# Layer 0 of a two-layer encoder: PSUM banks read earlier, the U product beside two gate groups, the Fourier transform between the other two

## The chip, the cores and the metric

One NeuronCore of a Trainium2 chip runs the whole computation. The metric is the device time of one execution in microseconds, as the median of several runs.

## The reference

Two layers (`DEPTH = 2`) over 512 positions of width 2048, in float32. Each layer normalises `x`, scales and shifts it by a vector that a large matrix `w_ada` makes of `c`, and multiplies by `w_in`. The columns of that product are: `u_f` (1024, the input of a Fourier mixing), `z_f` (1024, its gate), `cq` (512) and `ckv` with a rotary key (256 + 64) for latent attention, and `z_a` (1024, the attention's gate).

```python
h = _layernorm(x) * (1.0 + scale[:, None, :]) + shift[:, None, :]
u_f, z_f, cq, ckv, k_r, z_a = jnp.split(h @ w_in[l], split_pts, axis=-1)
y_f = _fourier_mix(u_f, w_fmix[l]) * jax.nn.silu(z_f)
...
y_a = _mla_attention(q_nope, q_rope, k_nope, k_rope, v) * jax.nn.silu(z_a)
y = jnp.concatenate([y_f, y_a], axis=-1) @ w_out[l]
x = _layernorm(DEEPNORM_ALPHA * x + gate[:, None, :] * y, ln_g[l], ln_b[l])
```

## The kernel before

**Precision.** Every operand of a large product is held as a high and a low part. `split` (L148) makes them: ScalarE (ACT) casts the value (L149), VectorE (DVE) subtracts the cast from the value (L150). `mm3` (L152) multiplies with three matmuls (L153 to L155). Attention's small operands are made in the same way by `scaled` (L427, L428).

**Weights.** `Stream` (L56) holds the weights as a list of units in the order of use. A unit is loaded by a DMA that SyncE (SP) issues into one of three `wr` buffers and then converted; `st.ahead(raw, conv)` says how many units are loaded and converted ahead of the one in use. A `dense` unit is 256 rows of 512 columns, one cast and one subtraction of 1024 columns. A `fold_unit` (L390) is 128 rows of the 1024 `u_f` columns: DVE adds and subtracts mirrored columns (L404, L405), ACT casts, DVE subtracts (L150) and adds to a running row (L415); `first_eo` (L621), which belongs to it, prepares the matching rows of the activations (ACT L624, DVE L625 and L626, a split of 512 columns). All converted tiles, sums and activations share 35 slots of the pool `bp`.

**Layer 0.** The vector of `w_ada` is needed before `h` exists, so layer 0 runs over the 16 blocks of 128 rows of `w_in` in five steps of 1, 2, 3, 4 and 6 blocks (`SZ`, L88), while DVE works the `w_ada` sums (L250) beside them. In each step `k_group` (L1079) runs over six column groups: CQ, CKV, two of `z_f` (ZF) and two of `z_a` (ZA). A group fills four PSUM banks, and these are then read: copied by ACT in the first step (L1099), added to a sum in SBUF by DVE afterwards (L1101). CQ alone stays in PSUM over the steps. PSUM has eight banks: four named `pa`, four named `pm`.

**The last step** (six blocks, three pairs a group) has the order CQ, CKV, ZA, ZA, ZF, ZF. Beside the four gate groups runs the product U (`u_step`, L714): one step for each of 16 fold units, 24 matmuls of 252 or 260 columns into the four `pm` banks. `UPAT` (L104) says how many U steps follow each of the twelve pairs: two in the first group, four in the second, five in the third, five in the fourth. Each group's sums then go through SiLU and are spilled to DRAM by SP (`spill`). Ahead of the fourth group `next(lq)` and `next(lkv)` read the two latents back from DRAM (`lat`) and rotate the key.

**Behind the last step** (L1142 to L1155) stand: `u_finish`, which splits the four `pm` banks of U; `folded_constants`, which makes the Fourier constants with twelve full-precision matmuls (L550); the transposes of the latents (L862); and then, alternating, the Fourier transform (`fourier_folded`, 14 steps on the `pm` banks) and the rotary part of the queries (`rotary_queries`, eight tiles). `project(0)` makes keys, values and queries of the first two heads, and the attention loop follows.

**What sets the order.** The program is written as one sequence. A planner at build time ranks each instruction by its place in that sequence, simulates the engines, and gives each engine a fixed order: the instruction of the lowest rank whose operands and buffers its simulation has ready. On the chip each engine takes its instructions in that order. `tc.high_priority(offset=n)` ranks instructions as if they had been written n instructions earlier.

Of the kernel before, what the change touches and what calls it, by code (L numbers as in the profile page):

```python
# [21 lines left out]
NT = S // P  # L22
# [60 lines left out]
def trunk_kernel(ctx: ExitStack, tc: tile.TileContext, x, c, positions, w_ada, b_ada, w_in, q_norm,  # L83
# [17 lines left out]

    FW, UAH, UA0, YS = 2, 6, 3, 4

    UPAT = [0, 1, 1, 2, 1, 1, 2, 2, 1, 2, 1, 2]  # L104


    XE, RN0, PL, WL = 8, 2, 1, 2
# [322 lines left out]
    def wq_unit(l, h0, nh, off, n):  # L430
        def load():
            t = wraw([P, 4, nh, n])
            for k in range(4):
                SP.dma_start(t[:, k], w_q_b[l, k * P:(k + 1) * P, :].rearrange(
                    "p (h c) -> p h c", c=192)[:, h0:h0 + nh, off:off + n])
            return t.rearrange("p k h c -> p k (h c)")

        def conv(t):
            s = [big([P, 2, 2, nh * n]) for _ in range(2)]
            for k in range(4):  # L440
                scaled(s[k // 2][:, 0, k % 2], s[k // 2][:, 1, k % 2], t[:, k], gcol(l, k))
            return lambda a, k: s[k // 2][:, a, k % 2]
        return Unit(load, conv)
# [27 lines left out]
    for l in range(DEPTH):  # L471
        if l == 0:
            for k0, nk in STEPS:
                last, m, ku = k0 + nk == NK, 0, 0
                for g in LAST if last else FIRST:
                    for k, n in pairs(k0, nk):
                        st.add(dense(w_in[l], k * P, *g, n))
                        if last and g in ZA + ZF:
                            for _ in range(UPAT[m]):
                                st.add(fold_unit(w_in[l], ku, lambda k: first_eo(k)))  # L480
                                ku += 1
                            m += 1
            for k in range(2):
                st.add(wq_unit(l, 4 * k, 4, 128, 64))
        else:
            add_groups(w_in[l], [ZA[0], ZF[0]])
            for k in range(NK):
                st.add(fold_unit(w_in[l], k))
            add_groups(w_in[l], [ZF[1], CQ, CKV])
            for k2 in range(8):  # L490
                if k2 in (0, 4):
                    st.add(wq_unit(l, k2, 4, 128, 64))
                st.add(dense(w_in[l], k2 * 256, *ZA[1]))
        for h0 in range(0, H, 2):
            st.add(wkv_unit(l, h0))
            st.add(wq_unit(l, h0, 2, 0, 128))
        add_groups(w_out[l], [(c0, 512) for c0 in range(0, D, 512)])
        ends.append(len(st.units))

# [161 lines left out]
    for l in range(DEPTH):  # L661
# [315 lines left out]
            while pending:  # L977
                pending.pop(0)()

        def project(h0):  # L980
            wv = st.next()
            for tp in range(2):
                v = big([P, 2, 2, 256])
                ps = pa()
                for t_ in range(2):
                    tb = tp * 2 + t_
                    ts = slice(tb * P, (tb + 1) * P)
                    o = ps[:, t_ * 256:t_ * 256 + 256].rearrange("p (h c) -> p h c", h=2)
                    for k in range(2):
                        mm3(o, ckv[k][:, 0, ts], ckv[k][:, 1, ts], wv(0, k)[:, :, 1], wv(1, k)[:, :, 1],  # L990
                            k == 0, k == 1)
                split(v[:, 0], v[:, 1], ps.rearrange("p (t c) -> p t c", t=2))
                for t_ in range(2):
                    for hd in range(2):
                        vs[h0 + hd, tp * 2 + t_] = v[:, :, t_, hd * P:(hd + 1) * P]
            wq = st.next()
            for hd in range(2):
                hs = slice(hd * P, (hd + 1) * P)
                ps = pa()
                for k in range(2):  # L1000
                    mm3(ps, wv(0, k)[:, hd, 0], wv(1, k)[:, hd, 0], ckv[k][:, 0], ckv[k][:, 1], k == 0, k == 1)
                t = big([P, 2, S])
                split(t[:, 0], t[:, 1], ps)
                ks[h0 + hd] = t
                ps = pa()
                for k in range(4):
                    mm3(ps, wq(0, k)[:, hs], wq(1, k)[:, hs], cq[k][:, 0], cq[k][:, 1], k == 0, k == 3)
                t = big([P, 2, S])
                scaled(t[:, 0], t[:, 1], ps, SCALE)
                qs[h0 + hd] = t  # L1010
# [57 lines left out]
        if l == 0:  # L1068

            for step, (k0, nk) in enumerate(STEPS):  # L1070
                final = k0 + nk == NK
                if step > 0:
                    finish_late()
                for k in range(k0, k0 + nk) if step else ():
                    h[k] = make_h(0, xT[k // 2][:, k % 2], k)
                left = [0 if final else float(sum(NK // (1024 // (256 * n)) for n in chunks(STEPS[step + 1][1])))]
                pace = left[0] / (6.0 * len(pairs(k0, nk)) * LEADS[step])

                def k_group(g, banks, work=lambda: None):  # L1079
                    n = g[1]  # L1080
                    k00, k01 = (0, NK) if g == CQ else (k0, k0 + nk)
                    for k, nr in pairs(k0, nk):
                        w = st.next()
                        p_ = min(pace, left[0])
                        left[0] -= p_
                        bg_step(p_ if p_ > 0 else ZP if not final else ZL if g in (CQ, CKV) else 0)
                        if g in ZF or g in ZA:
                            fm_half(banks, w, h, k, k == k00, k + nr == k01)
                        else:
                            tm_half(banks, w, h, k, n, k == k00, k + nr == k01)  # L1090
                        work()
                    if g == CQ:
                        return banks
                    if k0 == 0:
                        sums[g] = [big([P, 2, n], F32) for _ in range(2)]
                    s_ = [sums[g][tb // 2][:, tb % 2] for tb in range(NT)]
                    for tb in range(NT):
                        if k0 == 0:
                            A.copy(s_[tb], banks[tb][:, :n])  # L1099
                        else:  # L1100
                            V.tensor_tensor(s_[tb], s_[tb], banks[tb][:, :n], op=ALU.add)  # L1101
                    return s_

                if step == 0:
                    keep = [pa() for _ in range(NT)]
                if not final:
                    for i, g in enumerate(FIRST):
                        k_group(g, keep if g == CQ else [pm() for _ in range(NT)])
                        if step == 0 and i == 3:
                            cos_t, sin_t = rotary_tables()  # L1110
                    continue

                def pas():
                    return [pa() for _ in range(NT)]

                lq = latent_q(k_group(CQ, keep))
                next(lq)
                lkv = latent_kv(k_group(CKV, pas()))
                next(lkv)
                finish_late()  # L1120
                st.ahead(4, UA0)
                ub, ku, todo_u = None, 0, iter(UPAT)

                def u_steps():
                    nonlocal ub, ku
                    for _ in range(next(todo_u)):
                        if ub is None:
                            ub = u_start()
                        u_step(ub, ku)
                        ku += 1  # L1130

                for i, (g, dst) in enumerate(zip(LAST[2:], (0, 1, 2, 3))):
                    if i == 3:
                        next(lq)
                        next(lkv)
                        raw = constants_raw(0)
                    zs = k_group(g, pas(), u_steps)
                    for j in range(4):
                        A.activation(zs[j], zs[j], AF.Silu)
                    spill(dst, zs)  # L1140
                st.ahead(4, 2)
                u = u_finish(ub)  # L1142
                cw, nq, dt = folded_constants(0, raw)
                drain(lq)
                drain(lkv)
                fb, rq = fourier_folded(u), rotary_queries(1)
                for i in range(8):
                    next(fb, None)
                    next(rq, None)
                    next(fb, None)  # L1150
                drain(fb)
                gt = gates()
        else:
            unfolded(first_group(), 0)
# [24 lines left out]
            next(rq)  # L1179
            unfolded(fm_group(last, G1), 4)  # L1180
            drain(lkv)
        project(0)
        drain(rq)
        todo = [(hd, qh) for hd in range(H) for qh in range(2)]
        es, pts = {}, {}
# [161 lines left out]
```

## Time and profile before

| | us |
|---|---|
| median of three runs | 1429.53 (1428.49 to 1431.82) |
| the profiled execution | 1431.62 |
| its span, first to last instruction | 1429.8 |

| stretch of the span | us |
|---|---|
| steps of layer 0 but the last | 31 to about 222 |
| last step: CQ and CKV | to 246.6 |
| last step: the four gate groups with U | 246.6 to 373 |
| `u_finish`, constants, Fourier, rotary queries, first projections | 373 to 449.7 |
| attention of layer 0 and output projection | 449.7 to about 720 |
| layer 1 | to 1429.8 |

How to read it: TensorE (PE) is the engine with the most work. What counts is where it has idle time and which engine's instruction ends each idle stretch. A matmul's listed duration is longer than its share of PE's time, since matmuls overlap; the distance from start to start is what one costs. The same holds in a small way for DVE.

### The profile page before, as it was taken

The page shows a single profiled execution, that of the slowest core. Times are in us where ns is not written, and L with a number is a line of the kernel's source. Part 1 is how long each engine was busy: PE and PEld are TensorE (multiplying, and loading weights), DVE is VectorE, ACT ScalarE, POOL GpSimd, SP SyncE. Part 2 cuts the span into 40 slices and gives each one's busy share as a digit, 9 for nine tenths or more (in the row PEclk, how much of TensorE's full clock was granted, in tenths as well). Part 3 has the DMA queues.
Part 4 walks back from the last instruction along what each step waited for, and adds up shares of the span by engine and source line. Part 5 has one row for each costly group of instructions (what it writes and reads, how often), then busy time and mean ns, then how long its engine had stood idle before and what let it go on. Part 6 is the DMA issues. An engine that isn't in the chain of part 4 may idle for free. (4 is left out here: it accounts for less than half of the span.)

```text
span 1429.8 us, 19111 instructions
## 1 busy us (share of the span) xinstructions
PE 1326.3 (93%) x7029; PEld 1129.9 (79%) x7029; DVE 1041.0 (73%) x1744; ACT 602.3 (42%) x1135; POOL 59.7 (4%) x95
## 2 busy tenths in 40 slices
PE   4889899989898999999997998998999999999996
PEld 3768788878677888787776887887898888888885
DVE  7799993996689898689888748447655577733448
ACT  6521333754536776211157524323134577722110
POOL 1000000000100000000031001011100000000001
PEclk9999999999999999999998998999999999999998
DMA  8889853656466346989736435349734321272312
GB/s 275 294 277 321 296 206 113 192 180 184 147 227 223 118 148 202 328 299 319 271 113 214 161 99 155 89 147 337 247 93 110 111 66 46 59 259 89 103 59 118
DMA packets 137077, 260.88 MB, mean 182 GB/s; under 512 B 19788, under 2 KB 51672, under 8 KB 136984
## 3 DMA queue, kind: packets, MB, share of 16 engines
q1 hardware_dynamic: 129944, 236.33, 50.5%
q0 software_dynamic: 7040, 23.34, 4.7%
q8 instruction: 55, 0.90, 0.3%
q14 instruction: 38, 0.31, 0.1%
HBM read 241.12 MB, written 18.50 MB: 182 GB/s over the span
## 5 line engine op out<-in xcount | busy, mean ns | idle before, releaser
L153 PE MATMUL pa<-b,b 128*128 128x512 f32 (+2 forms) x1344 | 509.8, 381 | 33.2 <-ACT b L149 13.7
L154 PE MATMUL pa<-b,b 128*128 128x512 f32 (+2 forms) x1344 | 508.6, 379 | 5.1 <-DVE ln_v L190 5.1
L155 PE MATMUL pa<-b,b 128*128 128x512 f32 (+2 forms) x1344 | 506.5, 378 | 0.5 <-DVE b L150 0.5
L153 PEld LDWEIGHTS pa<-b,b 128*128 128x128 f32 x1344 | 256.1, 191 | 82.7 <-ACT b L149 19.9
L154 PEld LDWEIGHTS pa<-b,b 128*128 128x128 f32 x1344 | 257.9, 192 | 46.5 <-DVE ln_v L190 5.3
L149 ACT CAST b<-wr 128x1024 fp32r<-128x1024 f32 (+3 forms) x166 | 162.4, 989 | 313.1 <-PE pa L155 158.2
L155 PEld LDWEIGHTS pa<-b,b 128*128 128x128 f32 x1344 | 257.3, 192 | 46.8 <-DVE b L150 2.4
L150 DVE TENSOR_TENSOR b<-wr,b 128x1024 fp32r<-128x1024 f32 (+3 forms) x166 | 188.8, 1145 | 133.2 <-PE pa L154 61.0
L250 DVE SCALAR_TENSOR_TENSOR acc<-ada,cact,acc 128x1024 f32<-128x1024 f32 (+2 forms) x193 | 226.9, 1183 | 22.5 <-DMA ada<-in_w_ada_dram 20.6
L153 PE MATMUL pm<-b,b 128*128 128x256 f32 (+5 forms) x692 | 221.5, 320 | 8.3 <-DVE b L1101 3.7
L154 PE MATMUL pm<-b,b 128*128 128x256 f32 (+5 forms) x692 | 215.8, 312 | 0.0
L155 PE MATMUL pm<-b,b 128*128 128x256 f32 (+5 forms) x692 | 215.7, 312 | 0.0
L153 PEld LDWEIGHTS pm<-b,b 128*128 128x128 f32 x692 | 132.8, 192 | 21.0 <-issue 8.6
L154 PEld LDWEIGHTS pm<-b,b 128*128 128x128 f32 x692 | 133.1, 192 | 6.9
L155 PEld LDWEIGHTS pm<-b,b 128*128 128x128 f32 x692 | 132.9, 192 | 6.6
L150 DVE TENSOR_TENSOR b<-pm,b 128x512 fp32r<-128x512 f32 (+6 forms) x120 | 66.1, 574 | 38.8 <-ACT b L149 38.3
L149 ACT CAST b<-pm 128x512 fp32r<-128x512 f32 (+5 forms) x120 | 56.6, 499 | 65.4 <-PE pm L770 29.4
L149 ACT CAST b<-b 128x1024 fp32r<-128x1024 f32 (+1 forms) x48 | 43.3, 912 | 46.9 <-DVE b L405 29.0
L150 DVE TENSOR_TENSOR b<-b,b 128x1024 fp32r<-128x1024 f32 (+1 forms) x48 | 49.6, 1044 | 15.3 <-ACT b L149 15.3
L149 ACT CAST b<-t 128x512 fp32r<-128x512 f32 (+1 forms) x81 | 40.8, 530 | 40.3 <-DVE t L1059 15.2
L150 DVE TENSOR_TENSOR b<-t,b 128x512 fp32r<-128x512 f32 (+1 forms) x81 | 45.2, 578 | 9.3 <-ACT b L149 9.3
L1027 ACT ACTIVATE t<-t,ssum 128x512 f32<-128x512 f32 x64 | 45.3, 735 | 1.7 <-DVE ssum L1026 1.7
(180 smaller groups left out, 1247.6 us busy)
## 6 DMA issues: line engine op xcount, KB each, us to landing
wr<-in_w_in_dram SPq DMA_DIRECT2D x107, 512.0 KB, 4.0
ada<-in_w_ada_dram SPq DMA_DIRECT2D x96, 512.0 KB, 5.9
wr<-in_w_out_dram SPq DMA_DIRECT2D x64, 512.0 KB, 4.8
ada<-in_w_ada_dram SPq DMA_DIRECT2D x96, 256.0 KB, 5.1
ada<-in_w_ada_dram POOLq DMA_DIRECT2D x32, 512.0 KB, 5.1
b<-in_x_dram SPq DMA_DIRECT2D x16, 512.0 KB, 6.1
t<-szd SPq DMA_DIRECT2D x32, 256.0 KB, 4.1
ada<-in_w_ada_dram SPq DMA_DIRECT2D x32, 192.0 KB, 4.0
```

The source lines that it names most:

```text
L149: A.copy(hi, src)
L150: V.tensor_tensor(lo, src, f(hi), op=ALU.subtract)
L153: PE.matmul(o, lh, rh, start=first, stop=False)
L154: PE.matmul(o, lh, rl, start=False, stop=False)
L155: PE.matmul(o, ll, rh, start=False, stop=last)
L250: V.scalar_tensor_tensor(out=a, in0=t[:, r - r0], scalar=cact[:, r:r + 1], in1=a, op0=ALU.mult, op1=ALU.add)
L1027: A.activation(e, e, AF.Copy, scale=ssum)
```

## The change

Five things, all but the last two in the last step of layer 0:

- The reads of the PSUM banks at the end of every `k_group` stand in `tc.high_priority(offset=300)`. This holds in all five steps.
- `UPAT` is 2, 3, 3, 3, 3, 2: all 16 U steps follow the six pairs of the two ZA groups.
- `u_finish` and `folded_constants` stand ahead of the first ZF group (with `st.ahead(4, 2)`), the constants' DMAs one group earlier; after each of the six pairs of the ZF groups come two steps of the Fourier transform. The rest of it stands between the transposes of the latents.
- The rotary queries no longer alternate with the Fourier transform. One step stands ahead of `project(0)`, four inside it, the rest behind it.
- The second unit of rotary query weights moves behind the first pair of projection units. `project(0, rq)` holds for layer 1 too, where one last step of `rq` is left by then.

```diff
-    UPAT = [0, 1, 1, 2, 1, 1, 2, 2, 1, 2, 1, 2]
+    UPAT = [2, 3, 3, 3, 3, 2]
+    EV = 300
...
-                        if last and g in ZA + ZF:
+                        if last and g in ZA:
...
-            for k in range(2):
-                st.add(wq_unit(l, 4 * k, 4, 128, 64))
+            st.add(wq_unit(l, 0, 4, 128, 64))
...
+            if l == 0 and h0 == 0:
+                st.add(wq_unit(l, 4, 4, 128, 64))
...
-        def project(h0):
+        def project(h0, other=iter(())):
             wv = st.next()
             for tp in range(2):
+                next(other, None)
...
             for hd in range(2):
+                next(other, None)
...
-                    for tb in range(NT):
-                        if k0 == 0:
-                            A.copy(s_[tb], banks[tb][:, :n])
-                        else:
-                            V.tensor_tensor(s_[tb], s_[tb], banks[tb][:, :n], op=ALU.add)
+                    with tc.high_priority(offset=EV):
+                        for tb in range(NT):
+                            if k0 == 0:
+                                A.copy(s_[tb], banks[tb][:, :n])
+                            else:
+                                V.tensor_tensor(s_[tb], s_[tb], banks[tb][:, :n], op=ALU.add)
...
+                fb = None
                 for i, (g, dst) in enumerate(zip(LAST[2:], (0, 1, 2, 3))):
+                    if i == 1:
+                        raw = constants_raw(0)
+                    if i == 2:
+                        st.ahead(4, 2)
+                        fb = fourier_folded(u_finish(ub))
+                        cw, nq, dt = folded_constants(0, raw)
                     if i == 3:
                         next(lq)
                         next(lkv)
-                        raw = constants_raw(0)
-                    zs = k_group(g, pas(), u_steps)
+                    zs = k_group(g, pas(), u_steps if i < 2 else runner(fb, 2))
...
-                st.ahead(4, 2)
-                u = u_finish(ub)
-                cw, nq, dt = folded_constants(0, raw)
+                next(fb, None)
                 drain(lq)
+                next(fb, None)
                 drain(lkv)
-                fb, rq = fourier_folded(u), rotary_queries(1)
-                for i in range(8):
-                    next(fb, None)
-                    next(rq, None)
-                    next(fb, None)
                 drain(fb)
+                rq = rotary_queries(1)
+                next(rq)
                 gt = gates()
...
-        project(0)
+        project(0, rq)
         drain(rq)
```

## Rows read from the trace of the kernel before

**Rows 1.** The page: busy time of each engine, share of the span, instructions.
```profile
PE 1326.3 (93%) x7029; PEld 1129.9 (79%) x7029; DVE 1041.0 (73%) x1744; ACT 602.3 (42%) x1135; POOL 59.7 (4%) x95
```

**Rows 2.** Waits of PE, 225 to 460 us: total, times, longest.
```profile
PE pa L153 <- DVE b L1101: 9.3, 3, 3.8
```

**Rows 3.** Timeline of PE, last step: start, duration, instruction, idle before it.
```profile
246.60 0.39 PE L153 MATMUL pa<-b,b 128*128 128x512 f32 x1
...
257.51 0.28 PE L153 MATMUL pm<-b,b 128*128 128x260 f32 x1
...
260.33 0.39 PE L153 MATMUL pa<-b,b 128*128 128x512 f32 x1
...
265.82 0.28 PE L153 MATMUL pm<-b,b 128*128 128x260 f32 x1
```

**Rows 4.** Timeline of PE, where the second ZA group and the ZF groups start.
```profile
303.12 0.77 PE L153 MATMUL pa<-b,b 128*128 128x512 f32 x1 [3.78 <-DVE b L1101]
...
308.28 0.40 PE L153 MATMUL pa<-b,b 128*128 128x512 f32 x1
...
339.59 0.76 PE L153 MATMUL pa<-b,b 128*128 128x512 f32 x1 [3.33 <-DVE b L1101]
...
345.70 0.40 PE L155 MATMUL pa<-b,b 128*128 128x512 f32 x1
```

**Rows 5.** Stretch of 10 us: PE, PEld, DVE, ACT, POOL busy; granted clock, DMA, GB/s.
```profile
300.00:310.00 10.00, 6.88 (x20) 5.57 (x21) 8.53 (x12) 5.67 (x10) 0.00 (x0) 0.66 0.72 215
```

**Rows 6.** Waits of PE, 373 to 391 us (first and last of five).
```profile
PE pm L755 <- ACT b L149: 2.9, 1, 2.9
...
PE pm L862 <- DVE fc L558: 0.4, 1, 0.4
```

**Rows 7.** Waits of PE, 391 to 450 us (first two and last of six).
```profile
PE pa L153 <- DVE b L150: 2.4, 1, 2.4
PE pm L970 <- ACT b L427: 2.3, 1, 2.3
...
PE pm L153 <- issue: 0.5, 1, 0.5
```

**Rows 8.** Timeline of PE: the first instruction of the attention scores.
```profile
449.71 0.39 PE L1019 MATMUL pa<-b,b 128*128 128x512 f32 x1
```

**Rows 9.** Timeline of DVE beside the ZA groups.
```profile
250.22 0.42 DVE L625 TENSOR_TENSOR t<-t 128x256 f32<-128x256 f32 x1
...
262.31 1.22 DVE L150 TENSOR_TENSOR b<-wr,b 128x1024 fp32r<-128x1024 f32 x1
...
264.05 0.68 DVE L404 TENSOR_TENSOR b<-wr 128x504 f32<-128x504 f32 x1
...
268.35 0.68 DVE L404 TENSOR_TENSOR b<-wr 128x504 f32<-128x504 f32 x1
...
271.95 1.88 DVE L1101 TENSOR_TENSOR b<-b,pa 128x512 f32<-128x512 f32 x3
```

**Rows 10.** Timeline of DVE: a wait for the latents, one behind a spill, bank reads.
```profile
330.40 0.19 DVE L872 TENSOR_TENSOR t<-b,cos_t 128x32 f32<-128x32 f32 x1 [6.08 <-DMA b<-lat]
...
348.34 0.68 DVE L404 TENSOR_TENSOR b<-wr 128x504 f32<-128x504 f32 x1 [2.09 <-DMA szd<-b]
...
363.57 0.69 DVE L1101 TENSOR_TENSOR b<-b,pa 128x512 f32<-128x512 f32 x1 [2.83 <-PE pa L155]
364.94 0.69 DVE L1101 TENSOR_TENSOR b<-b,pa 128x512 f32<-128x512 f32 x1 [0.69 <-PE pa L155]
```

**Rows 11.** Busy time by stretch: layer 1's group with the Fourier steps between its pairs.
```profile
922.00:985.00 63.00, 62.97 (x332) 53.23 (x331) 37.17 (x63) 17.78 (x35) 8.96 (x17) 1.00 0.56 186
```

**Rows 12.** DVE by line and shape, 371 to 450 us: count, busy, mean ns.
```profile
L250 DVE SCALAR_TENSOR_TENSOR acc<-ada,cact,acc 128x1024 f32<-128x1024 f32 x18 | 23.0, 1279 | 0.0
```

**Rows 13.** Busy time by stretch, attention and output projection (first, last of four).
```profile
450.00:500.00 50.00, 49.97 (x297) 43.71 (x296) 44.78 (x83) 39.12 (x84) 0.00 (x0) 1.00 0.46 153
...
600.00:700.00 100.00, 96.59 (x432) 78.26 (x432) 90.78 (x98) 17.90 (x17) 0.00 (x0) 1.00 0.89 315
```

**Rows 14.** Waits of PE, 0 to 240 us: the steps before the last.
```profile
PE pm L153 <- DVE b L1101: 3.7, 3, 2.0
```

## The prediction

> **What bounds the kernel now.** I read the page's busy times first: PE is busy 93% of the span, DVE 73% [rows 1]. So the question for any part of this kernel is where PE stands idle. I then took the waits of PE in the stretch that the change rewrites, and the timelines of PE and DVE there. In this stretch, from the first ZA matmul at 246.60 [rows 3] to the first score at 449.71 [rows 8], 203.1 us long, the losses are of three kinds.
>
> First, the starts of the second, third and fourth gate group wait for the bank reads of the group before: 9.3 us in three waits [rows 2]. PE has only four `pa` banks, and the reader sees why the reads are late: DVE has the conversions of units ahead in front of them. After the two longer waits the clock is down. [...] The twelve matmuls from 303.12 to 308.28 took 5.16 us [rows 4]. At full clock a dense pair of 24 matmuls takes 265.82 - 260.33 = 5.49 us [rows 3], 0.229 each, so twelve take 2.75: 2.4 us lost. From 339.59 to 345.70 [rows 4] it is 14 matmuls in 6.11 instead of 3.2: 2.9 us. Together these starts cost 9.3 + 5.3 = 14.6 us.
>
> Second, behind U, 373 to 391 us: five kinds of waits, 2.9 us for the split of U's banks and down to 0.4, sum 6.0 [rows 6]. Nothing else was left for PE there.
>
> Third, 391 to 450 us, the Fourier steps beside the rotary queries: six kinds, 2.4 and 2.3 down to 0.5, sum 9.2 [rows 7].
>
> From 450 us PE is busy 49.97 of 50 us [rows 13], so what is saved before that shifts everything after it.
>
> **The change, part by part.**
>
> *Group starts (gain 13.5).* The ranks move the bank reads ahead of conversions, and the new pattern puts three U steps behind the last pair of the first ZA group and two behind that of the second. A U step is 260.33 - 257.51 = 2.82 us [rows 3], so the reads have 8.5 and 5.6 us of PE work over them and need four times 1.88 / 3 = 0.63 us [rows 9], 2.5 us. Both waits go, with their clock loss. The start of the second ZF group has two Fourier steps over it, and DVE there has the latents behind the reads now: its 6.08 us wait for them [rows 10] stays but holds up no fold unit. I leave 1 us. Bounds: 9.3 (the clock falls elsewhere) to 14.6.
>
> *U in half the time (loss 6.5).* This is the part that costs. PE's work for the two ZA groups is 6 x 5.49 + 16 x 2.82 = 78.1 us: from 246.60 to 324.7. DVE takes 268.35 - 264.05 = 4.30 us for one fold unit with its activations, back to back [rows 9]. So it needs 16 x 4.30 = 68.8, five dense units of 1.22 and eight bank reads of 0.63: 79.9 us. It gets to them at 250.22 [rows 9], behind the latents; the first fold unit now stands one place nearer in the stream, and I take its 4.30 as done by then, in DVE's idle time beside CKV. That gives 250.22 + 75.6 = 325.8 and 2.82 for the last U step: 328.6, 3.9 us behind PE's own. DVE becomes the bound here, so each wait of DVE now counts. For bank reads that reach the head of DVE's queue early I add 2.7 us (four gaps of 0.69 [rows 10]). Sum 6.6, taken as 6.5. Bounds: 0 (more fold work done early) and 14 (the 2.83 and three gaps of 0.7, 4.9 us, in both groups).
>
> [...]
>
> *U's end and the constants under dense work (gain 5).* The 6.0 us of rows 6 now have pairs of the first ZF group beside them, two of which are converted ahead (11 us of PE). Their DVE work, some 16 us from 373 to 389, stands in front of the third pair's conversion: I leave 1 us. The DMAs that move with it (the constants' on SP and POOL, one group earlier) stand behind the first ZA group's spill, with a whole group to land; POOL is 4% busy [rows 1]. Cost nothing; without that cover, the 2.9 us wait once. Bounds 3 to 7.5.
>
> *Fourier between dense pairs (cost 0).* Layer 1 already does this, two steps after each pair: there PE is busy 62.97 of 63 us [rows 11]. Cost 0 to 2.
>
> *The rest behind the last step (gain 3).* Left are the transposes, eight rotary tiles and the first projections, some 33 us of PE work: the stretch's 203.1 less 14.6, 6.0, 9.2 and some 2 of clock is 171; off go ZA's 78, the ZF pairs' 6 x 5.49 = 33, the Fourier steps' 63 - 8 x 5.49 = 19 (layer 1's group [rows 11] less its eight pairs) and, as an estimate, 8 for U's end and the constants, two thirds of the 12 us that PE had left of the 18 of rows 6. The rotary chain (PE, six DVE instructions, ACT, DVE, PE) has less beside it than now. Of the 11 us (waits and clock) I take 8 as left. Bounds: -2 (2.4 us at each of the last five of its steps is 12, against 11) to +8.
>
> *Work that fills DVE's holes.* Between 371 and 450 us DVE does 18 `w_ada` sums of attention's own, 23.0 us [rows 12]. With fewer holes some of them move into the attention, where DVE has 5.2 us idle in the first 50 and 9.2 in the last 100, 32 us of 250 in all [rows 13]. Cost nothing; if that cover is gone, up to 3 us. The later `wq` unit is four DMAs on SP that move behind two others: nothing waits for its heads until the third projection.
>
> *The earlier steps (gain 1.5).* Three waits of 3.7 us are of the same kind [rows 14]. DVE is nearly full there, and a step's start waits for DVE's `w_ada` sums anyway, so I take under half. Bounds: -1.3 (one sum of 1.28 [rows 12] late at a step's end) to 3.7. Layer 1's one moved step: nothing.
>
> Sum: 13.5 - 6.5 + 5 + 3 + 1.5 = 16.5 us. The profiled execution took 1431.62 with a span of 1429.8; by this it would take 1415.1, span 1413.3. It lay 2.1 above the median of the runs, so against the median, 1429.53, I expect **1413.0**.
>
> **The rivals.**
>
> *DVE stands in front of the banks.* The planner's simulated PE and the real one differ, so reads ranked first may be queued well ahead of their matmuls, with all conversions behind them. Price: 4.9 us in each ZA group, 9.8 instead of 2.7, and the gain of the tail lost too: 16.5 - 7.1 - 3 = 6.4, 1423.1. For it: rows 10. Against: those gaps came where DVE had little else. [...]
>
> *All is hidden.* DVE starts more fold work beside CQ and CKV, and the tail gains its 8: 16.5 + 4.5 + 5 = 26, 1403.5. Against: only two units are converted ahead before the ZA groups.
>
> *Slower: fold units wait for slots.* 16 fold units of four slots each pass through the pool while sums are still being spilled. Before, one such wait held DVE 2.09 us behind a spill [rows 10], at five U steps a group; now there are eight. In a stage that DVE bounds it goes straight to PE: 16.5 / 2.09 = 8 such waits eat the gain, and one at each of 16 units gives 33.4 - 16.5 = 17 us more, 1446.5. Against: the rows show two such waits, not eight.
>
> *It doesn't do what it says.* If the ranks change no order, the reads stay behind the backlog that the fold units now make larger, and the group starts cost what they do: 16.5 - 13.5 - 1.5 = 1.5, 1428.0.
>
> **How the numbers follow.** A measurement of this kernel can tell about 0.2%, 2.9 us, from no change. Chances: forecast 0.50 (1407 to 1420), DVE in front of the banks 0.17, all hidden 0.15, slots 0.09, no effect 0.09. Faster 0.50 + 0.17 + 0.15 = 0.82; same 0.09; slower 0.09. The range reaches from just under the all-hidden case to beyond the case of blocked DVE and leaves the last two out: 1402 to 1427.
>
> **What would show it.** Right: no wait of PE on bank reads (L1101) over 1 us from 246 us on; DVE over 95% busy in the two ZA groups, which end near 331; the waits on L755 gone; PE without gaps between the ZF pairs; the first score near 433. Wrong: DVE idle before L1101 in the ZA groups (first rival), DVE waiting for spills before L404 (third), or waits of PE on L970 that grow past 11 us behind the ZF groups.

## The result, and the profile after

The changed kernel took 1439.51 us, median of 8 runs (1435.97 to 1445.4), against 1431.21 for the kernel before in the same comparison: ratio 1.0059, 95% interval 1.0035 to 1.0083. It is slower by 0.6%, where 1413.0 was forecast. The profiled execution took 1441.51 us with a span of 1439.7.

The page's busy line of the changed kernel, against [rows 1]:

```profile
PE 1326.0 (92%) x7029; PEld 1132.1 (79%) x7029; DVE 1042.7 (72%) x1744; ACT 602.5 (42%) x1135; POOL 59.9 (4%) x95
```

The same work, 9.9 us more span: PE stands idle more, or is granted less clock. Where, the stretches tell. The next view is the table by stretch of the changed kernel (start:end and length in us; then busy us and instructions of PE, PEld, DVE, ACT and POOL, the granted clock, the DMA share and GB/s):

```profile
243.00:334.00 91.00, 82.01 (x533) 74.79 (x532) 81.61 (x131) 52.70 (x112) 4.90 (x9) 0.94 0.54 158
334.00:401.00 67.00, 60.68 (x298) 47.76 (x297) 50.50 (x127) 26.93 (x66) 2.14 (x4) 0.95 0.78 257
401.00:429.00 28.00, 25.86 (x170) 22.57 (x169) 27.02 (x62) 16.46 (x38) 0.00 (x0) 1.00 0.68 214
429.00:460.00 31.00, 15.06 (x74) 12.98 (x73) 17.27 (x43) 8.25 (x20) 0.00 (x0) 0.63 0.49 151
460.00:500.00 40.00, 39.97 (x224) 35.32 (x225) 29.49 (x60) 31.28 (x67) 0.00 (x0) 0.94 0.24 70
```

These are the ZA groups; the ZF groups with U's end and the Fourier steps; the rest of the transform with the first rotary tiles; the last five rotary tiles; the attention. The fourth stands out: PE idle for 16 of 31 us, and the granted clock at 0.63 of full speed, so that part of the 15 busy us ran below it: from 452 to 458.2 us the granted clock was 0.50. [rows 13] shows what PE does in attention once nothing holds it.

Up to 429 us the change had paid. ZA began at 243.14 (246.60 before, [rows 3]); the first score was at 424.14 instead of 449.71 [rows 8]. At 429 us the changed kernel still had some 7.7 us of rotary work on PE that the other had behind it, all but a last set of transposes, at its first score, and had some 4 us of scores done already. By this estimate it was 449.71 - (429 + 7.7 - 4), some 17 us, ahead. At the start of layer 1 it was 8.9 us behind (749.57 against 740.68), and stayed there.

The waits of PE in the changed kernel, to be held against [rows 2, 6, 7] (engine, line, waited for; total us, times, longest). From 243 to 334 us, the ZA groups:

```profile
PE pa L155 <- DVE b L1107: 7.2, 1, 7.2
PE pm L156 <- DVE b L152: 1.7, 3, 0.9
```

from 334 to 429 us (two smaller ones left out):

```profile
PE pm L758 <- ACT b L151: 4.6, 1, 4.6
PE pm L865 <- DVE b L152: 1.0, 1, 1.0
PE pa L155 <- DVE b L152: 1.0, 1, 1.0
PE pa L155 <- ACT b L151: 0.7, 1, 0.7
```

and from 429 to 460 us (one of 0.8 left out):

```profile
PE pm L973 <- DVE t L430: 15.1, 5, 3.6
```

L973 holds the transposes of a rotary tile, and L430 the second half of the split that makes their input. PE's timeline there shows a beat (start us, us, operation, and in brackets the idle time before and what ended it):

```profile
426.41 0.46 PE L973 MATMUL pm<-identr,t 128*128 128x128 f32 x4
...
428.21 0.40 PE L1024 MATMUL pa<-b,b 128*128 128x512 f32 x1
...
433.16 0.51 PE L973 MATMUL pm<-identr,t 128*128 128x128 f32 x4 [3.63 <-DVE t L430]
...
439.89 0.52 PE L973 MATMUL pm<-identr,t 128*128 128x128 f32 x4 [2.89 <-DVE t L430]
...
446.02 0.72 PE L973 MATMUL pm<-identr,t 128*128 128x128 f32 x4 [3.23 <-DVE t L430]
...
452.12 0.72 PE L973 MATMUL pm<-identr,t 128*128 128x128 f32 x4 [2.69 <-DVE t L430]
...
458.22 0.72 PE L973 MATMUL pm<-identr,t 128*128 128x128 f32 x4 [2.69 <-DVE t L430]
```

One tile every 6.1 to 6.7 us. At full clock (granted 1.00 in 426 to 429 us) the transposes and the twelve matmuls of a tile are 428.21 - 426.41 = 1.8 us of PE. From 433.16 to 458.22 PE's order is: transposes of tile i-1, twelve matmuls of tile i, transposes of tile i, and nearly nothing else; each set of transposes waits for its tile's way through DVE (L961 to L966), ACT (L429) and DVE (L430). In the first turn two `w_ada` sums of 1.28 us stand on DVE between the tile's instructions; in the last two DVE has the chain alone, and the wait is still 2.69. Four such tiles, a fifth set of transposes (0.5) and the last two matmuls of a score block (0.46) make 8.2 us of work in 31: about 23 us lost.

### The profile page after: what moved, and what is told of

The parts are those of the page before. It is cut to its first block, busy times and chain, and to the rows that moved or that the text cites. A ratio compares the mean times of both kernels' runs of the same rounds, so it can differ in the third digit from the quotient of the medians.

```text
span 1439.7 us, 19109 instructions
## 1 busy us (share of the span) xinstructions
PE 1326.0 (92%) x7029; PEld 1132.1 (79%) x7029; DVE 1042.7 (72%) x1744; ACT 602.5 (42%) x1135; POOL 59.9 (4%) x95
## 5 line engine op out<-in xcount | busy, mean ns | idle before, releaser
L151 ACT CAST b<-wr 128x1024 fp32r<-128x1024 f32 (+3 forms) x166 | 162.4, 990 | 316.0 <-PE pa L157 171.9
L152 DVE TENSOR_TENSOR b<-wr,b 128x1024 fp32r<-128x1024 f32 (+3 forms) x166 | 188.7, 1144 | 132.9 <-PE pa L156 61.1
L152 DVE TENSOR_TENSOR b<-pm,b 128x512 fp32r<-128x512 f32 (+5 forms) x120 | 65.4, 572 | 35.6 <-ACT b L151 35.0
L151 ACT CAST b<-pm 128x512 fp32r<-128x512 f32 (+5 forms) x120 | 56.1, 499 | 52.3 <-PE pm L773 22.0
L151 ACT CAST b<-b 128x1024 fp32r<-128x1024 f32 (+1 forms) x48 | 43.3, 912 | 47.5 <-DVE b L407 32.4
L152 DVE TENSOR_TENSOR b<-b,b 128x1024 fp32r<-128x1024 f32 (+1 forms) x48 | 49.5, 1042 | 16.5 <-ACT b L151 14.0
L151 ACT CAST b<-t 128x512 fp32r<-128x512 f32 (+1 forms) x81 | 40.8, 530 | 34.7 <-DVE t L1064 15.1
L152 DVE TENSOR_TENSOR b<-t,b 128x512 fp32r<-128x512 f32 (+1 forms) x81 | 45.0, 576 | 6.4 <-ACT b L151 6.4
L1030 ACT ACTIVATE t<-pa,mx 128x512 f32<-128x512 f32 x64 | 44.2, 696 | 5.3 <-DVE mx L1027 5.2
```

Source lines behind the costliest of these rows:

```text
L151: A.copy(hi, src)
L152: V.tensor_tensor(lo, src, f(hi), op=ALU.subtract)
L1030: A.activation(e, ps, AF.Exp, bias=mx, accum_out=ssum)
```

## The experiments

All ratios are against the kernel before, measured beside it. "Changed kernel" is 1.0059.

| run | what it is | us | ratio, 95% interval |
|---|---|---|---|
| rq_only | before, with the rotary order alone | 1452.47 | 1.0151 (1.0111 to 1.0192) |
| ev0 | changed, without the ranks | 1446.21 | 1.0091 (1.0056 to 1.0125) |
| spread | changed, rotary tiles among the attention | 1424.34 | 0.9947 (0.993 to 0.9964) |
| own_tiles | changed, rotary buffers of their own | 1423.47 | 0.9942 (0.992 to 0.9965) |
| lag | changed, transposes one tile later | 1421.34 | 0.9923 (0.9894 to 0.9952) |
| combo | spread and lag | 1413.13 | 0.9872 (0.9844 to 0.99) |
| ua1 | combo, one unit converted ahead | 1411.01 | 0.9853 (0.9818 to 0.9888) |
| ufin | ua1, U's end behind a dense pair | 1399.92 | 0.978 (0.9749 to 0.981) |
| ufin_again | the same kernel once more | 1403.59 | 0.9813 (0.9796 to 0.983) |
| reads_first | ufin, one order on DVE | 1400.51 | 0.9783 (0.9762 to 0.9803) |

### Is it the rotary tail? rq_only, lag, spread

**rq_only** makes the one move in the kernel before: the transform is drained first, and the rotary tiles, projections and the later `wq` unit stand as in the changed kernel.

```
...
-                fb, rq = fourier_folded(u), rotary_queries(1)
-                for i in range(8):
-                    next(fb, None)
-                    next(rq, None)
-                    next(fb, None)
-                drain(fb)
+                drain(fourier_folded(u))
+                rq = rotary_queries(1)
+                next(rq)
...
```

> The kernel before, with one part of the change: the rotary queries no longer alternate with the Fourier steps but stand ahead of, inside and behind the first projections; U and the Fourier transform stay where they were, and bank reads keep their rank. Theory A: the same serial tail as in the changed kernel appears, about 22 us, less the 3 to 5 us of waits on rotary transposes that the Fourier stretch had; it has more waits of its own without them: 1446 to 1456, ratio 1.011 to 1.018. Theory B: rotary work only changes places, within 3 us of before, ratio 0.998 to 1.002.

It cost 1.5%, more than the whole change does. PE's wait on the transposes is there (L971 is the same line in this kernel), and the stretch 430 to 460 has PE busy 16.75 of 30 us at a clock of 0.72:

```profile
PE pm L971 <- DVE t L428: 17.8, 6, 4.4
```

So the rest of the change gained beside it: from 1.0151 to 1.0059.

**lag** writes the transposes of tile i behind the matmuls of tile i+1.

```
-                    while pending:
+                    while len(pending) > (l == 0):
                         pending.pop(0)()
```

> The changed kernel, with the transposes of rotary tile i written behind the matmuls of tile i+1 instead of ahead of them, in layer 0; all else as it is. Theory A (the tail is a serial chain because the matmuls of a tile stand behind the transposes of the tile before on PE): a tile's period falls from 6.1 us to the 4 to 4.5 us that DVE, ACT and the transposes take without the matmuls, over four or five tiles 6 to 10 us: 1429 to 1434, ratio 0.998 to 1.002. Theory B (ZA groups): no change, 1437 to 1441.

It gave 18 us by the medians (ratio 1.0059 to 0.9923), about twice what was expected; the wait fell from 15.1 to 5.7 us:

```profile
PE pm L973 <- DVE t L430: 5.7, 2, 4.7
```

The rest fits the clock: with a tile's matmuls to do during another tile's way through DVE and ACT, PE was busy 24.08 of 30 us in 430 to 460, and the granted clock there was 0.89, against 0.63 in 429 to 460 of the changed kernel; behind it, from 460 us, it was 1.00 and not 0.94. How the 18 us divide was not tried.

**spread** doesn't drain the rotary tiles behind the first projections, but takes one step of them behind each pair of score blocks.

```
         project(0, rq)
-        drain(rq)
+        if l == 1:
+            drain(rq)
 ...
                 es[i] = scores(hd, qh)
+                next(rq, None)
```

> The changed kernel, with the rotary tiles that are left behind the first projections taken one at a time inside the attention loop (one step behind each pair of score blocks) instead of all at once ahead of it. Theory A, the rotary tail: in the changed kernel's trace PE gets from 428.7 to 459.8 us only 8.6 us of work done, since the last four rotary tiles come one after another with nothing between them; then about 20 us come back and the time is 1417 to 1422, ratio to before 0.990 to 0.994. Theory B, the loss lies in the ZA groups, where DVE is the bound: no change from the changed kernel, 1437 to 1441, ratio 1.004 to 1.008.

1424.34, 15 us less by the medians where theory A expected about 20. Two of five waits are left:

```profile
PE pm L973 <- DVE t L430: 6.5, 2, 3.6
```

Taken together, **combo**:

> The changed kernel with both edits to the rotary tail: steps spread over the attention loop, and each tile's transposes behind the next tile's matmuls. Theory A: the two waits on rotary transposes that each edit alone left (6.5 and 5.7 us, with some 3 us of low clock) go: 1412 to 1417, ratio 0.986 to 0.990. Theory B (what is left of the tail is DVE's own pace): no better than the better one alone, 1420 to 1424, ratio 0.992 to 0.995.

1413.13, and no wait on L973 is left. PE is busy 40.00 of 40 us in 430 to 470:

```profile
430.00:470.00 40.00, 40.00 (x261) 35.90 (x261) 38.84 (x85) 33.19 (x76) 0.00 (x0) 1.00 0.51 158
```

That is the forecast's 1413.0, but by another kernel, the change with its tail repaired, and the match is chance: the forecast left 8 us of loss in this part, where combo has no wait on L973, and it had no wait of 7.2 us at the second ZA group and none of 4.6 at U's end, which combo still has.

### Why nothing filled the tail: own_tiles

Three score blocks of the attention were on PE before 429 us. Why did no other work follow? The changed kernel's ACT shows its first exp only at the tail's end:

```profile
458.93 0.69 ACT L1030 ACTIVATE t<-pa,mx 128x512 f32<-128x512 f32 x1
```

The exps and the rotary tiles take their temporaries from one pool of nine (`t2p`). **own_tiles** gives the three rotary temporaries a pool of their own and takes two buffers from `t2p`.

```
-    t2p = ctx.enter_context(tc.tile_pool(name="t2p", bufs=9))
+    t2p = ctx.enter_context(tc.tile_pool(name="t2p", bufs=7))
+    rqp = ctx.enter_context(tc.tile_pool(name="rqp", bufs=1))
 ...
-                qs_ = t2([P, 4, 64])
-                qt = t2([P, 4, 32])
+                qs_ = rqp.tile([P, 4, 64], F32, tag="rqs", name=nm("rqs"))
+                qt = rqp.tile([P, 4, 32], F32, tag="rqt", name=nm("rqt"))
 ...
-                qb = t2([P, 4, 2, 64], F32R)
+                qb = rqp.tile([P, 4, 2, 64], F32R, tag="rqb", name=nm("rqb"))
```

> The changed kernel with the rotary tiles' three temporaries in a pool of their own (one buffer each; the shared pool of temporaries goes from 9 to 7 buffers). Program order, PSUM and the drain ahead of the attention stay. Theory A1: the tail is empty because the shared pool hands out its buffers in the order of the program, so the first exponentials wait for the last rotary tile's buffer and the four score banks stay full; with a pool of its own PE has scores and the next projections between the rotary tiles: 1419 to 1427, ratio 0.991 to 0.997. Theory A2: the exponentials wait for something else (the activation table, the ranks), and the tail stays: 1436 to 1442, ratio 1.003 to 1.008.

1423.47, with one buffer for each of the three and seven instead of nine in the other pool. No wait on the rotary transposes (L974 there) stands in its list from 400 to 470 us, though other waits of 7.4 us in all do, and the first exp (L1031 there) runs at 430.61:

```profile
430.61 0.69 ACT L1031 ACTIVATE t<-pa,mx 128x512 f32<-128x512 f32 x1
```

So it was the shared pool that held the exps: the score banks filled, and PE had nothing left but the chain. The reading that fits is that the pool hands out its buffers in the order of the program, so that an exp's temporary stood behind those of the last rotary tile. spread agrees: it leaves the pool of nine as it is and only writes rotary tiles behind scores, and its first exp runs before three of its sets of rotary transposes, the last of which starts at 467.25.

```profile
442.16 0.69 ACT L1030 ACTIVATE t<-pa,mx 128x512 f32<-128x512 f32 x1
```

No run takes the order apart from the number of buffers, which is ten in all in own_tiles.

### The ranks: ev0

> The changed kernel with offset 0 in place of 300 at the bank reads, so their rank is where they are written. Theory A: in the last step DVE's order has the reads at the same places with either offset, so nothing changes there; in the steps before, the 3.3 us that the changed kernel is ahead at 94 us go: 1440 to 1444, ratio 1.006 to 1.010. The rival of the prediction (reads ranked early make DVE stand in front of the banks): faster than the changed kernel by 5 us or more, 1434 or less, ratio 1.002 or less.

The edit is `EV = 300` to `EV = 0`. By the ratios it cost 4.6 us (1.0091 against 1.0059), with intervals that overlap, so the times alone show no cost. The waits on the bank reads in the earlier steps, up to 240 us, are plainer:

```profile
PE pm L155 <- DVE b L1107: 6.4, 5, 1.7
```

against 1.5 us in two waits with the ranks. Up to the start of ZA, these waits are 1.3 to 2.6 us in the nine traces with the ranks and 3.7 to 6.4 in the three without (before, rq_only, ev0). When ZA begins says less: 247.78 here, 243.14 in the changed kernel, but 245.00 and 247.46 in ufin and ufin_again, two executions of one kernel with the ranks, and 244.65 in rq_only, which has none. In the last step nothing changes: the wait at the start of the second ZA group is 7.3 us without the ranks and 7.25 with them. So the first rival, reads that block DVE, is out (DVE itself waits 0.3 us at the reads of the changed kernel's last step), and of "it doesn't do what it says" the order in the ZA groups is what holds.

### The ZA groups: ua1 and reads_first

In the changed kernel the second ZA group starts late, and the clock is down behind it. PE's and DVE's timelines:

```profile
292.15 0.77 PE L155 MATMUL pa<-b,b 128*128 128x512 f32 x1 [7.25 <-DVE b L1107]
...
300.07 0.28 PE L155 MATMUL pm<-b,b 128*128 128x260 f32 x1
```

```profile
286.72 1.22 DVE L152 TENSOR_TENSOR b<-b,b 128x1024 fp32r<-128x1024 f32 x1
...
289.47 0.67 DVE L406 TENSOR_TENSOR b<-wr 128x504 f32<-128x504 f32 x1
290.06 0.67 DVE L407 TENSOR_TENSOR b<-wr 128x504 f32<-128x504 f32 x1
...
291.32 0.68 DVE L1107 TENSOR_TENSOR b<-b,pa 128x512 f32<-128x512 f32 x1
```

The first ZA group's last matmul into its banks began at 275.34; the first read began at 291.32, with DVE never idle between. The 24 matmuls of the pair took 300.07 - 292.15 = 7.92 instead of 5.49 us, at a granted clock of 0.68 (compare [rows 5]): 2.4 us of clock.

**ua1** converts one unit ahead in combo instead of three (`UA0` 3 to 1), to bring the reads forward.

> The last kernel with one number changed: weights are converted one unit ahead of their use beside the ZA groups instead of three. In DVE's fixed order the reads of the first ZA group's banks then stand behind nine and ten fold units' first instructions as before the last two of them, one fold unit (4.3 us) earlier for the first bank. Theory C: the 7.25 us wait and the low clock behind it (2.4 us) come from where the order was fixed, not from DVE's total work: the wait falls by 4.3 us or more and 3 to 8 us come back: ratio lower than the last kernel's by 0.002 to 0.006. Theory D: DVE's total work in the ZA groups is the bound; the wait moves to the U steps behind, ratio within 0.001 of the last kernel's.

The wait only fell to 6.9 us, and 1411.01 can't be told from combo. It doesn't decide.

**reads_first** tries it by force: with ufin as its base (below), all that the second ZA group converts is queued on DVE behind the last bank read of the first. ufin was measured again beside it.

```
...
+                    if i == 1:
+                        with tc.issue_after(last[0]):
+                            zs = k_group(g, pas(), u_steps)
...
```

> The kernel of ufin once more, beside reads_first: both theories expect about 1400 us (1397 to 1403), PE's wait for the first ZA group's bank reads at about 6.9 us near 293.6 and the granted clock down behind it (0.59 in 292 to 301).

> ufin with one more order on DVE: all conversions that the second ZA group starts are queued behind the last bank read of the first ZA group, so the reads stand behind the eight fold units that the group's own U steps need and not behind a ninth and the scaled rows (L628, L629) of four more. In ufin the ninth unit's and those rows' work fills DVE from 285.47 to 292.81, the first read's start. Theory order (the place of the reads on DVE is what PE waits for): the reads start near 285, the 6.9 us wait and the 2.4 us of low clock behind it fall to under 1.5 us together; DVE had some 5 us idle between 301 and 334 in ufin, so of the 9 us at least 5 are kept: 1391 to 1395. Theory total (DVE's work as a whole bounds the two groups, and any order only moves the wait): the wait on the reads goes, but waits on U's matmuls for split fold units (PE on DVE L152) take its place with 5 us or more, and the time stays within 2 us of ufin, 1398 to 1402.

The reads now run at 283.74, all four in a row; the wait of 6.9 us is gone, and the clock is 1.00 in 292 to 301 where it was 0.62:

```profile
283.74 2.47 DVE L1116 TENSOR_TENSOR b<-b,pa 128x512 f32<-128x512 f32 x4
```

But PE's waits for split fold units (L152), 1.8 us in ufin_again, grew; its waits from 240 to 332 us are

```profile
PE pm L156 <- DVE b L152: 4.4, 6, 1.0
PE pa L155 <- DVE b L1116: 1.1, 1, 1.1
PE pm L155 <- ACT b L151: 0.7, 1, 0.7
```

The two tables by stretch of the ZA groups, reads_first and then ufin_again, from the first ZA matmul to the first ZF matmul:

```profile
244.46:331.16 86.70, 80.54 (x530) 72.76 (x529) 79.96 (x128) 50.73 (x109) 5.69 (x11) 1.00 0.52 159
```

```profile
247.46:336.76 89.30, 80.67 (x531) 73.64 (x529) 81.61 (x130) 53.07 (x112) 4.90 (x9) 0.96 0.55 161
```

The groups are 2.6 us shorter, the idle time of PE 6.2 instead of 8.6 us. (In ufin's own trace they take 335.46 - 245.00 = 90.5 us, so 2.6 is the smaller of two differences.) The gain does not last. From the first ZF matmul to the latents' first transpose reads_first takes 391.8 - 331.16 = 60.6 us, ufin_again 57.0 and ufin 56.0: reads_first has a wait of 1.1 us at U's end (L758) there that they don't have, and a granted clock of 0.86 in 334 to 346 us, where ufin_again has 1.00. Why was not tried. Its median is 3.1 us below ufin_again's, with intervals that overlap, and 0.6 above ufin's. No gain of the whole kernel is shown.

So the place of the reads on DVE made the one long wait, but theory order was wrong about the time, 1400.51 where it had 1391 to 1395. Theory total has the time in its range; of the waits that it put in place of the long one, 5 us or more, 4.4 came, and more was lost behind the groups. That DVE's total work takes the gain back fits this and is not shown by itself. Two things stay open besides: why the planner's order had the reads there, and why PE's busy time in the groups stayed at 80.5 although the clock came back.

### U's end: ufin

In the changed kernel U's end runs after the ZA groups, with only three dense matmuls of the first ZF group between (PE's timeline):

```profile
339.10 0.80 PE L758 MATMUL pm<-b,t 128*128 128x256 f32 x2 [4.60 <-ACT b L151]
```

**ufin** writes U's end and the constants as the first step behind the first ZF pair.

```
-                        fb = fourier_folded(u_finish(ub))
-                        cw, nq, dt = folded_constants(0, raw)
+
+                        def behind():
+                            nonlocal_u = u_finish(ub)
+                            consts.extend(folded_constants(0, raw))
+                            yield
+                            yield from fourier_folded(nonlocal_u)
+
+                        fb = behind()
```

> The last kernel with U's end and the constants written behind the first pair of the first ZF group instead of ahead of it. PE's order then has all 24 dense matmuls ahead of the first product with the row sums, not three. Theory: the 4.6 to 5.0 us wait of that product was only a matter of its place; it goes, 4 to 7 us: ratio lower than the last kernel's by 0.003 to 0.005. Rival: the Fourier steps start later and their rest lengthens the stretch behind the ZF groups by as much: within 0.001.

1399.92, and 1403.59 the second time: 11 and 7 us less than ua1, where 4 to 7 were expected. The wait on L758 is gone. From the first ZF matmul to the latents' first transpose it is 391.5 - 335.46 = 56.0 us (57.0 the second time), in ua1 398.5 - 334.17 = 64.3; in 334 to 380 PE is busy 45.95 of 46 us at a clock of 1.00, in ua1 42.47 at 0.96. So 7 to 8 us lie there, of which 2.2 are the wait that ua1 had on L758; how the rest divides was not tried. This version is about 2% faster than the kernel before, in two measurements (0.978 and 0.9813).

## Why the prediction was wrong

**The step that failed** is "the rest behind the last step (gain 3)", with bounds of -2 to +8. Of 11 us that waits and clock cost there before, it left 8. The changed kernel lost about 23 in the tail, and behind it PE had the clock at 0.94 for 40 us, 2.4 more: some 25. So a gain of 3 was a loss of about 14, and this one term is 17 of the some 26 us between 1413.0 and 1439.51. It is also what turned the 17 us ahead at 429 us into 8.9 behind.

The prediction had the parts in hand. It named the chain (PE, six DVE instructions, ACT, DVE, PE) and wrote that it "has less beside it than now". But it priced the chain at "2.4 us at each of the last five of its steps". The wait of 2.4 us in [rows 7] is not the chain's: it is a projection's matmul (L153, at 441.64) that waits for a split. The rotary transposes (L970) waited 2.3 once for ACT, 1.6 once for a Fourier temporary, and for the end of their own chain only

```profile
PE pm L970 <- DVE t L428: 1.7, 3, 0.8
```

That is what is left of a wait while Fourier steps and projections stand between a tile's matmuls and its transposes. Uncovered it is 3 us a tile of pure wait, 15.1 in five, and the PE part of a tile nearly doubled besides: 6.10 - 2.69 = 3.4 us in the last turn, at a granted clock of 0.50 (452.12 to 458.22 us), where it is 1.8 at 1.00. rq_only shows the tail by itself, lag and spread repair it from both ends. (The lower bound is also mis-added: 12 against 11 is -1, not -2.)

The second half of the same step was never asked: what PE would do instead. "Some 33 us of PE work" for transposes, rotary tiles and projections read as if they filled each other. The attention stood ready to fill them, and own_tiles shows that it was kept out by buffers, not by data or rank. The sign "the first score near 433" was met, even early, at 424.14: scores then stood ahead of rotary tiles that were still to come, so the first of them no longer told how far the kernel was.

**Group starts (gain 13.5).** Two of three went as forecast: no wait on the reads at the starts of the ZF groups. At the second ZA group it came back as 7.25 us and 2.4 of clock, so that the term gave some 5 us. I gave the reads 8.5 us of U steps to hide under; they came 16 us after their bank, since DVE had about four fold units' time between.

**U in half the time (loss 6.5).** DVE as the bound was right in kind: PE's pure 78.1 us took 333.64 - 243.14 = 90.5, a loss of 12.4, of which 9.65 are the long wait and its clock, counted under group starts. In reads_first, without the long wait, it is 86.7, a loss of 8.6: the term was some 2 us too small there. The two can't be added, since DVE went on converting while PE waited (busy 15.98 of 15.98 us from 275.34 to 291.32). DVE was busy 81.61 of the 91 us from 243 to 334, 90% and not "over 95%": it lost 2.5 us to a spill (the "slots" rival's wait, once) and some 5 in gaps of 0.5 to 1.1 in the second group, most of them for ACT's half of a split (L151). "No wait of PE on bank reads (L1101) over 1 us" was wrong because of that one wait.

**U's end and the constants (gain 5).** The longest wait of [rows 6] went from 2.9 to 4.6 us at the same place (L755, now L758), not away, and the clock was at 0.69 in 334 to 345 us. The two pairs that should have covered it stood behind it in PE's order. ufin moves it behind the first pair, and the stretch is 7 to 8 us shorter than in ua1, more than the 5 that I gave the cover.

**Fourier between dense pairs (cost 0)** held within the 2 us given: waits of 0.6, 0.7 and 0.5 us are all that stands there. The two of 1.0 lie behind it, at the latents' transposes and at 417 us.

**The earlier steps (gain 1.5).** The reads' waits fell from 3.7 to 1.5 us [rows 14], and ev0 says the ranks do this. ZA began 3.5 us earlier, but not by these waits: PE's idle time up to there is 37.3 us before and 37.2 after, and one kernel, ufin's, begins ZA 2.5 us apart in two executions. So a gain of time is not shown.

**The rivals.** DVE in front of banks: out by ev0. What the traces show is the other way round, with conversions in front of reads: in the changed kernel the first ZA group's last bank matmul began at 275.34 and its first read at 291.32; in reads_first, which queues the reads first, they began at 283.74, after a last bank matmul at 276.68. DVE kept to the planner's order throughout: in the traces of before and of the changed kernel its 1736 instructions (the page's 1744 less eight reads of an accumulator) stand line for line in the order of the program. Slots: the one wait of 2.5 us for a spill, not eight (the rows of the kernel before show one such wait, too, where the prediction says two). The slower rival thus had the right sign and the wrong mechanism; the sentence that did hold was the last of the prediction, "waits of PE on L970 that grow past 11 us behind the ZF groups": that line is L973 now, with 15.1.

## What to carry to other kernels

When a change moves dense work away from beside a serial chain, a wait read under the old cover is no price for the chain: add up one whole turn of it (here 6.1 to 6.7 us against 1.8 us of PE work), times the turns that are left bare, and look behind it for what the engine could do instead. Then ask of that filler whether it can start: buffers that it shares with the chain hold it back as surely as missing data. The cheap repairs are to lag the consumer by one turn, to scatter the turns among later work, or to give the chain buffers of its own.

## What the hardware showed that I had not expected

The clock made the bare chain dearer than its waits: of the about 23 us lost in the tail, 15.9 are waits. With gaps of 2.7 to 3.2 us in each turn of six, PE was granted 0.52 of full speed from 440 to 460 us of the changed kernel:

```profile
440.00:460.00 20.00, 10.57 (x53) 9.60 (x53) 7.17 (x24) 6.77 (x16) 0.00 (x0) 0.52 0.30 89
```

Beside shorter gaps the clock stayed up: reads_first has six waits of 0.3 to 1.0 us on split fold units in its ZA groups, and in 292 to 301 us, with PE busy 6.70 of 9 us, the clock stayed at 1.00:

```profile
292.00:301.00 9.00, 6.70 (x48) 5.93 (x48) 8.34 (x15) 5.54 (x13) 0.00 (x0) 1.00 0.43 125
```

Beside one wait of 6.9 us in ufin_again, in the same stretch, it was 0.62. With 6.2 us idle in eight waits the two groups took 86.70 us there, and with 8.6 us in four, the long one among them, 89.30 in ufin_again. PE's busy time was 80.54 and 80.67, so a gain from the clock itself is not shown in them, and the whole kernel was no faster.
